# A two-layer hybrid encoder on one core: packed S5 preparation, layer 1's tables made beside other products, more half products, another order of steps

## The chip, the cores and the metric

The kernel runs on one core of one Trainium2 chip. The metric is the device time of one execution in microseconds (us). TensorE (PE in the profile) does the matrix products, VectorE (DVE), ScalarE (ACT) and GpSimd (POOL) the element-wise work, SyncE (SP) issues most of the DMAs and ScalarE the others.

## The reference, cut to what matters

```python
D_MODEL = 1024; SEQ = 512; DEPTH = 2; D_FF = 4 * D_MODEL
...
    lam_bar = jnp.exp(lam * step)                       # S5: 2 directions x 16 groups x 64 states
    b_bar = ((lam_bar - 1.0) / lam)[..., None] * b_c    # complex, (..., 16)
    bu = jnp.einsum('zgph,blgh->zblgp', b_bar, u.astype(jnp.complex64))
...
    for l in range(DEPTH):
        mix = hybrid_mixer(x, ...)      # x @ w_in, then S5, GLA, windowed attention, then @ w_out
        x = layer_norm(DEEPNORM_ALPHA * x + mix, ln1_g[l], ln1_b[l])
        hid = jnp.square(jax.nn.relu(x @ w_ff1[l]))
        x = layer_norm(DEEPNORM_ALPHA * x + hid @ w_ff2[l], ln2_g[l], ln2_b[l])
    return x
```

All data are float32. The S5 part is a diagonal complex recurrence in both directions; the kernel computes it in blocks of 8 steps with tables of powers of `lam_bar`, which depend on the parameters alone.

## The kernel before, in words

**Products.** A float32 product is made as three products of a fast 32-bit format (`mm3`, L250 to L252): each operand is split into a high and a low half. For weights `wunit` (L242 to L246) loads one 128x1024 unit into a buffer `raw` on SP's queue, copies the high half with ACT (L219) into one of six places of `WA`, and subtracts for the low half on DVE or POOL (L246). PE's products wait for that subtraction.

**A layer.** x stands in `XR` (512 tokens x 1024), transposed and split in `XT` (shown as XTP, XTQ, XTR). The input projection goes in four groups: wg1 (S5's u, GLA's values), g0 = wg0 (GLA's q, k and gates), g2 and g3 (attention). Then come the three mixers, the product with w_out in two halves (`out_half0`, `out_half1`), LayerNorm (`layer_norm`), the feed-forward part and a second LayerNorm.

**S5.** `tb_params` makes the powers of `lam_bar` up to 8, the factor (lam_bar-1)/lam (`QRI`) and the table `PS2` for both layers on DVE, at the start of the kernel. `tables(l)` goes over four groups j: it loads B and C (`BC`) and a second table (`CBK`), makes B times the factor (`BB`, six DVE operations of 128x64, L572 to L577), multiplies both with the powers (L587 to L595, each 128x512; for layer 0 the second of the two sets on POOL for j = 0 to 2), transposes on PE (`wst`, L599), writes one table to `scr_out` in HBM (L603), forms the block table on PE (`lag`, L607 to L613) and, after the last j, writes it to `scr_lag` in 15 small DMAs (L619, L621). `turns(l)` fills the rotation table `ROT`. `s5_u`, `s5_states`, `s5_scan` and `s5_out` use the tables.

**Feed-forward.** Chunk c (0 to 3) has eight tiles of 128 hidden units (`ff1`), then the product with w_ff2 in two halves. A plain tile is 24 matmuls of 128x512. From tile `CFG["st"][l]` on (12 in layer 0, 4 in layer 1), two tiles are made as a pair in seven products of halves (`ff1_pair`, 84 matmuls of 128x256, shown as f1s): its two weight tiles are loaded straight into `MA` (L1054, L1055), sums of their halves are made on DVE (L228) and split like other weights (ACT L219, DVE L1073).

**Order.** Within an engine the order is fixed when the program is built, by a list scheduler that takes the steps of the strings in `CFG["seq"]` as priorities. Layer 1's tables and turns are issued behind tile 3 of layer 0's chunk 0, at lower priority than what stands behind:

```python
            if l == 0 and c == 0:
                with tc.issue_after(state[CFG["tf"]].ins):
                    run(tables(1))
                    turns(1)
```

They use parts of `MA` and `MB`. Each queue (SP's and ACT's) issues its DMAs in order, and an issue that waits holds up what stands behind it. In the rows, `sc`, `pT` and `so` are attention's scores, transposed probabilities and outputs; `sy`, `zT`, `glg`, `glv` are the end of S5; `go`, `goT` the end of GLA.

Of the kernel before, what the change touches and what calls it, by code (L numbers as in the profile page):

```python
# [63 lines left out]
def trunk(tc, I, out, dbg=None):  # L64
# [299 lines left out]
    def tb_params():  # L364
# [3 lines left out]
        ST = [vs[:, 512:640], vs[:, 1536:1664]]  # L368
        tmps, IT = vs[:, 672:1024], vs[:, 1984:2048].bitcast(I32)
# [55 lines left out]
        V.tensor_scalar(e1, e1, -2.0, 1.0, op0=MUL, op1=ADD)  # L425
        V.tensor_copy(RW[:, 0], e1)
# [15 lines left out]

        tb = [t.rearrange("p (g k) -> p g k", g=32) for t in ST]

        def powers(W, b):
            def at(k):
                return W[:, 0, :, b + k], W[:, 1, :, b + k]
            for k, i, j in ((2, 1, 1), (3, 2, 1), (4, 2, 2)):
                cmul(*at(k), at(i), at(j))
            a4r, a4i = bc(W[:, 0, :, b + 4], 2, 4), bc(W[:, 1, :, b + 4], 2, 4)  # L450
            lo, hi_ = slice(b + 1, b + 5), slice(b + 5, b + 9)
            V.tensor_tensor(tb[0], W[:, 0, :, lo], a4r, op=MUL)
            V.tensor_tensor(tb[1], W[:, 1, :, lo], a4i, op=MUL)
# [11 lines left out]
        nr, (rr, ri) = t32(), (QRI[:, 0], QRI[:, 1])  # L465
        V.tensor_scalar(nr, PW[:, 0, :, 1], -1.0, None, op0=ADD)
        ni = PW[:, 1, :, 1]
        V.tensor_tensor(u1, are, are, op=MUL)
        V.tensor_tensor(u2, aim, aim, op=MUL)
        V.tensor_tensor(u1, u1, u2, op=ADD)  # L470
        V.reciprocal(e4, u1)
        V.tensor_tensor(u1, nr, are, op=MUL)
        V.tensor_tensor(u2, ni, aim, op=MUL)
        V.tensor_tensor(rr, u1, u2, op=ADD)
        V.tensor_tensor(rr, rr, e4, op=MUL)
        V.tensor_tensor(u1, ni, are, op=MUL)
        V.tensor_tensor(u2, nr, aim, op=MUL)
        V.tensor_tensor(ri, u1, u2, op=SUB)
        V.tensor_tensor(ri, ri, e4, op=MUL)
# [9 lines left out]
        unit_(wc, ws)  # L489
# [11 lines left out]
    def turns(l):  # L501

        t = [MA[:, 1024 * i:1024 * i + 1024] for i in range(2)]
        V.tensor_copy(ROT[:, :, :, 0], RW[:, :, 16 * l:16 * l + 16])
        k = 1
        while k < 64:
            n = 32 * k
            t1, t2 = [x[:, 0:n].rearrange("p (r g k) -> p r g k", r=2, g=16) for x in t]
            x = ROT[:, :, :, 0:k]
            wr, wi = [bc(bc(ROT[:, r, :, k - 1], 1, 2), 3, k) for r in range(2)]  # L510
            V.tensor_tensor(t1, x, wr, op=MUL)
            V.tensor_tensor(t2, x, wi, op=MUL)
            V.tensor_tensor(ROT[:, 0, :, k:2 * k], t1[:, 0], t2[:, 1], op=SUB)
            V.tensor_tensor(ROT[:, 1, :, k:2 * k], t1[:, 1], t2[:, 0], op=ADD)
            k *= 2
            if k == 8:
                unit_(ROT[:, 0, :, 7], ROT[:, 1, :, 7])

    def tables(l):
        nb = 2 if l == 0 else 1  # L520
        vs = M.yc[:, 2048:4096] if l == 0 else None
        areas = [MA, M.lt, MB] if l == 0 else [MA[:, 0:3072], MA[:, 5120:6656], MA[:, 3072:5120]]
# [12 lines left out]
        if l == 0:  # L535
            CBKs = [reg(512) for _ in range(nb)]
            BCs = [TAB[:, 256 * i:256 * i + 256] for i in range(4)]
# [16 lines left out]
        BCs = [c.rearrange("p (w r g h) -> p w r g h", w=2, r=2, g=4) for c in BCs]
# [472 lines left out]
    def ff_act(ps, i):  # L1027
# [12 lines left out]
        if i in (3, 4, 5, 7):  # L1040
            state["ff%d" % i] = ins
# [315 lines left out]
```

## Time and profile before

| what | value |
|---|---|
| median of 3 runs | 1258.68 us (1257.42 to 1258.88) |
| the profiled execution's own time | 1256.86 us |
| its span, first to last instruction | 1255.0 us |
| PE busy | 1182.3 us, 94% of the span |
| DVE, ACT, POOL busy | 888.9, 558.8, 150.4 us |
| mean granted TensorE clock | 0.973 of full speed |
| layer 0: input projection and mixers | about 0 to 240 us |
| layer 0: w_out, LayerNorm, feed-forward, LayerNorm | about 240 to 671 us |
| layer 1: the same two parts | about 671 to 845, 845 to 1255 us |

The span is what the profile covers; 1.9 us lie outside it. An engine's busy time is time in which it ran an instruction; the rest of the span it waited. PE's 94% is a mean over stages: in the feed-forward parts PE runs without a gap but one, in the mixers it waits in many small places. The granted clock says at what share of its full speed of 2.4 GHz TensorE's array ran.

### The profile page before, as it was taken

Reading aid. Unit: us, or ns where it says so; the run is one execution under the profiler, and the core shown is the slowest. Engines: PE = TensorE matmul, PEld = TensorE weight load, DVE = VectorE, ACT = ScalarE, POOL = GpSimd, SP = SyncE. Lnnn points to the kernel's source line nnn. Section 1 sums busy time; section 2 is a strip of 40 time slices with the busy share of each in tenths; the row PEclk is TensorE's granted clock in tenths of the full one; section 3 lists DMA queues with packets and bytes.
Section 4 is the critical chain, followed back from the end, with each engine's and each line's share of the span. In section 5 each row is a group of like instructions: output and inputs, shape, how many; then the busy total and the mean of one; then the engine's idle time right before and its main releaser. Section 6 shows DMA issues by size and latency. Waiting matters only on the chain.

```text
span 1255.0 us, 18704 instructions
## 1 busy us (share of the span) xinstructions
PE 1182.3 (94%) x7400; PEld 985.4 (79%) x7400; DVE 888.9 (71%) x1663; ACT 558.8 (45%) x939; POOL 150.4 (12%) x103
## 2 busy tenths in 40 slices
PE   6796899999999899999999999799999999999997
PEld 5685675668888788989987876456798898998986
DVE  8988768658876774856755278784997485764957
ACT  4262267525522442734623554572465272461640
POOL 3523112212000000000122131120300000000000
PEclk9898998999999899999999999899999999999999
DMA  6340430212442441421422414202144142250331
GB/s 221 107 143 9 122 106 1 80 56 76 134 160 97 146 148 42 143 85 53 131 103 57 161 60 102 84 17 84 35 138 148 51 146 74 87 164 19 101 119 67
DMA packets 50615, 121.67 MB, mean 97 GB/s; under 512 B 13280, under 2 KB 20320, under 8 KB 50528
## 3 DMA queue, kind: packets, MB, share of 16 engines
q1 hardware_dynamic: 37680, 103.53, 25.1%
q10 hardware_dynamic: 12848, 16.95, 4.9%
q8 instruction: 58, 0.95, 0.3%
q14 instruction: 29, 0.24, 0.1%
HBM read 110.53 MB, written 8.88 MB: 95 GB/s over the span
## 4 chain that ended last, share of the span: by engine, by line
PE 75%; DVE 16%; DMA 3%; ACT 2%; issue 2%; SPq 1%; ACTq 0%; POOL 0%; DVEq 0%
PE o L250 12%; PE o L251 11%; PE o L252 11%; PE f1s L250 6%; PE f1s L251 6%; PE f1s L252 6%; PE so L981 2%; PE proj L250 2%; PE proj L251 2%; PE proj L252 2%; PE pT L975 1%; PE f1e L251 1%; PE f1e L252 1%; PE f1e L250 1%; PE f L250 1%
## 5 line engine op out<-in xcount | busy, mean ns | idle before, releaser
L219 ACT ACTIVATE WA<-raw 128x1024 fp32r<-128x1024 f32 (+2 forms) x129 | 132.4, 1029 | 138.6 <-DMA raw<-in_w_ff 43.2
L246 DVE TENSOR_TENSOR WA<-raw,WA 128x1024 fp32r<-128x1024 f32 (+1 forms) x102 | 121.9, 1195 | 86.3 <-ACT WA L219 83.8
L219 ACT ACTIVATE WA<-MA 128x1024 fp32r<-128x1024 f32 (+1 forms) x72 | 64.6, 914 | 138.5 <-PE o L252 104.0
L992 DVE SCALAR_TENSOR_TENSOR XR<-XR,o 128x512 f32<-128x512 f32 (+1 forms) x81 | 52.9, 677 | 98.1 <-PE o L252 97.7
L1073 DVE TENSOR_TENSOR WA<-MA,WA 128x1024 fp32r<-128x1024 f32 (+1 forms) x72 | 74.5, 1043 | 16.5 <-ACT WA L219 16.5
L246 POOL TENSOR_TENSOR WA<-raw,WA 128x1024 fp32r<-128x1024 f32 (+2 forms) x27 | 62.0, 2301 | 173.0 <-ACT WA L219 162.1
L252 PE MATMUL f1s<-xs,WA 128*128 128x256 f32 x288 | 81.1, 281 | 0.0
L250 PE MATMUL f1s<-xs,WA 128*128 128x256 f32 x288 | 81.0, 281 | 0.0
L251 PE MATMUL f1s<-xs,WA 128*128 128x256 f32 x288 | 81.0, 281 | 0.0
L228 DVE TENSOR_TENSOR MA<-MA,f1s 128x256 f32<-128x256 f32 x120 | 49.1, 417 | 29.5 <-PE f1s L252 21.4
L228 POOL TENSOR_TENSOR XR<-XR,lt 128x512 f32<-128x512 f32 (+1 forms) x13 | 18.3, 1407 | 400.0 <-ACT XR L216 400.0
L250 PE MATMUL o<-WA,yYa 128*128 128x512 f32 (+1 forms) x162 | 64.4, 397 | 1.4 <-DVE XR L992 1.4
L250 PE MATMUL o<-WA,yQ 128*128 128x512 f32 (+1 forms) x164 | 64.2, 391 | 0.1
L251 PE MATMUL o<-WA,yQ 128*128 128x512 f32 (+1 forms) x164 | 64.1, 391 | 0.0
L250 PE MATMUL o<-WA,yP 128*128 128x512 f32 x160 | 63.8, 399 | 0.3 <-DVE yP L988 0.3
L251 PE MATMUL o<-WA,yYb 128*128 128x512 f32 (+1 forms) x162 | 63.8, 394 | 0.0
L252 PE MATMUL o<-WA,yYb 128*128 128x512 f32 (+1 forms) x162 | 63.6, 394 | 0.0
L250 PE MATMUL o<-WA,yYb 128*128 128x512 f32 (+1 forms) x162 | 63.5, 392 | 0.0
L251 PE MATMUL o<-WA,yYa 128*128 128x512 f32 (+1 forms) x162 | 63.5, 392 | 0.0
L252 PE MATMUL o<-WA,yYa 128*128 128x512 f32 (+1 forms) x162 | 63.5, 392 | 0.0
L252 PE MATMUL o<-WA,yQ 128*128 128x512 f32 (+1 forms) x164 | 63.4, 390 | 0.0
L251 PE MATMUL o<-WA,yP 128*128 128x512 f32 x160 | 63.4, 396 | 0.0
(456 smaller groups left out, 3534.2 us busy)
## 6 DMA issues: line engine op xcount, KB each, us to landing
raw<-in_w_ff SPq DMA_DIRECT2D x80, 512.0 KB, 3.4
MA<-in_w_ff SPq DMA_DIRECT2D x48, 512.0 KB, 3.5
raw<-in_wg SPq DMA_DIRECT2D x23, 512.0 KB, 3.5
raw<-in_w_out SPq DMA_DIRECT2D x16, 512.0 KB, 3.4
scr_out<-MA SPq DMA_DIRECT2D x8, 512.0 KB, 3.5
yc<-scr_out ACTq DMA_DIRECT2D x8, 512.0 KB, 4.8
raw<-in_wg SPq DMA_DIRECT2D x8, 288.0 KB, 2.8
MA<-in_s5cb ACTq DMA_DIRECT2D x8, 256.0 KB, 3.3
```

The costliest lines, as they stand in the source:

```text
L219: S.activation(out=o_, in_=i_, func=AF.Copy)
L228: eng.tensor_tensor(o_, a, b, op=op)
L246: (eng or V).tensor_tensor(WA[:, i, 1, c], raw[:, c], WAf[:, i, 0, c], op=SUB)
L250: T.matmul(ps, a[1], b[0], start=first, stop=False)
L251: T.matmul(ps, a[0], b[1], start=False, stop=False)
L252: T.matmul(ps, a[0], b[0], start=False, stop=last)
L975: T.transpose(ps[:, b * 128:b * 128 + 128], P[:, h, b * 128:b * 128 + 128], ident)
L981: T.matmul(ps[64 * v:64 * v + 64, :], av[:, tt - 1 + b0 + b, 64 * v:64 * v + 64], M.pT[v][:, b].rearrange("p h q -> p (h q)"), start=(b == ...
L992: V.scalar_tensor_tensor(x, x, scale, ps, op0=MUL, op1=ADD)
L1073: V.tensor_tensor(WA[:, u, 1, c], src, WAf[:, u, 0, c], op=SUB)
```

## The change

Four parts. (1) `tb_params` computes real and imaginary parts, and several powers, in one operation: the powers take 12 DVE operations of 64 to 256 columns where there were 24 of 32 and 128, the factor 14 where there were 16, and one correction (`unit_`, six operations) is left out. B and C of a layer come in one DMA of 512 KB, and the product with the factor is made for all groups at once: four DVE operations (two of 512, two of 256 columns) for 24 of 64. (2) Layer 1's tables are made in three parts: j = 0, 1 beside the second product of chunk 0, j = 2, 3 and the DMAs to `scr_lag` beside that of chunk 1, the turns beside that of chunk 2; they work in `MA[:, 2048:6656]` and `ROT`, and their turns in `MB`. (3) In layer 0 the pairs begin with tile 8: tiles 8 to 11 become two pairs. (4) The steps' order: layer 0 has `out` behind `scan` and `g3`, and `w3`, `y` ahead of `s5o`; layer 1 has `sink` ahead of `states`, and `out`, `y` behind `s5o`.

```diff
-    "st": [12, 4],
+    "st": [8, 4],
-    "seq": ["u g0 st0 tb st1 gates turns g2 scores states sink out scan g3 keys late w0 s5o w3 y w1 w2", "tb g0 u gates st0 st1 scan scores states sink g2 out g3 y keys late s5o w0 w2 w1 w3"],
+    "seq": ["u g0 st0 tb st1 gates turns g2 scores states sink scan g3 out keys late w0 w3 y s5o w1 w2", "tb g0 u gates st0 st1 scan scores sink states g2 g3 keys late s5o out w0 y w2 w1 w3"],
+    "td": [2, 2, 0, 0],
+    "tn": [0, 0, 7, 0],
...
+        def cmul(dst, a, br_, bi_):
+            t1, t2 = [v.rearrange("p r (g k) -> p r g k", g=32)[:, :, :, 0:a.shape[-1]] for v in (v1, v2)]
+            V.tensor_tensor(t1, a, br_, op=MUL)
+            V.tensor_tensor(t2, a, bi_, op=MUL)
+            V.tensor_tensor(dst[:, 0], t1[:, 0], t2[:, 1], op=SUB)
+            V.tensor_tensor(dst[:, 1], t1[:, 1], t2[:, 0], op=ADD)
+        for k in (1, 2, 4):
+            cmul(PW[:, :, :, k + 1:2 * k + 1], PW[:, :, :, 1:k + 1],
+                 *[bc(PW[:, r, :, k:k + 1].to_broadcast([128, 32, k]), 1, 2) for r in range(2)])
...
-        unit_(wc, ws)
...
-        areas = [MA, M.lt, MB] if l == 0 else [MA[:, 0:3072], MA[:, 5120:6656], MA[:, 3072:5120]]
+        areas = [MA, M.lt, MB] if l == 0 else [MA[:, 2048:6656], ROT.rearrange("p r g k -> p (r g k)")]
...
+        nc.scalar.dma_start(BC, I["s5bc"][l].rearrange("p (w r g h) -> p w r g h", w=2, r=2, g=16))
+        t3 = [t.rearrange("p (r g h) -> p r g h", r=2, g=16) for t in TT]
+        for t, q in zip(t3, (rr, ri)):
+            V.tensor_tensor(t, BC[:, 0], bc(bc(q, 1, 2), 3, 16), op=MUL)
+        V.tensor_tensor(BC[:, 0, 0], t3[0][:, 0], t3[1][:, 1], op=SUB)
+        V.tensor_tensor(BC[:, 0, 1], t3[0][:, 1], t3[1][:, 0], op=ADD)
         for j in range(4):
             yield j
...
-            V.tensor_tensor(t3[0], br, qr, op=MUL)
...
-            V.tensor_tensor(BB[:, 1], t3[0], t3[1], op=ADD)
...
-            if l == 0 and c == 0:
-                with tc.issue_after(state[CFG["tf"]].ins):
-                    run(tables(1))
-                    turns(1)
+            if l == 0:
+                if c == 0:
+                    tb1, tn1 = tables(1), turns(1)
+                with tc.issue_after(state["ff%d" % (8 * c + 7)].ins):
+                    for g, n in ((tb1, CFG["td"][c] + (c == 0)), (tn1, CFG["tn"][c])):
+                        if n:
+                            run(g, n)
```

**SP's queue in layer 0's feed-forward part, before.** `raw<-in_w_ff` are weight units (the 16 of one row: chunk 0's), `MA<-in_w_ff` the loads of the pairs, L603 and L619, L621 the tables' writes.

```order
33 L242 DMA raw<-in_w_ff 128x1024 x16
34 L603 DMA scr_out_95<-MA 128x1024
...
38 L603 DMA scr_out_95<-MA 128x1024 x2
39 L1054 DMA MA<-in_w_ff 128x1024
40 L619 DMA scr_lag_97<-MA 16x16x16 x2
41 L621 DMA scr_lag_97<-MA 16x16x16
...
53 L621 DMA scr_lag_97<-MA 16x16x16
54 L1054 DMA MA<-in_w_ff 128x1024
55 L1055 DMA MA<-in_w_ff 128x1024 x2
```

The same place in the changed kernel (the pairs' loads are L1030 and L1031, the tables' writes L580, L596 and L598):

```order
34 L244 DMA raw<-in_w_ff 128x1024 x8
35 L1030 DMA MA<-in_w_ff 128x1024
36 L1031 DMA MA<-in_w_ff 128x1024
37 L244 DMA raw<-in_w_ff 128x1024 x8
38 L580 DMA scr_out_95<-MA 128x1024 x2
39 L1031 DMA MA<-in_w_ff 128x1024
...
47 L244 DMA raw<-in_w_ff 128x1024 x7
48 L580 DMA scr_out_95<-MA 128x1024 x2
49 L1030 DMA MA<-in_w_ff 128x1024 x2
50 L1031 DMA MA<-in_w_ff 128x1024
51 L596 DMA scr_lag_97<-ROT 16x16x16 x2
...
64 L598 DMA scr_lag_97<-ROT 16x16x16
65 L1031 DMA MA<-in_w_ff 128x1024
```

The first pair's two loads now stand ahead of chunk 0's second weights and of every write of the tables, and the 15 writes to `scr_lag` have moved behind three of the four loads of chunk 2's first two pairs.

**DVE at the start, before**, from the last small operations of `tb_params` (L486 to L488) to the end of the first group's tables; the row of L246 with 576 columns is the third split of wg0.

```order
132 L577 TENSOR_TENSOR MB<-yc 128x64
133 L485 SCALAR_TENSOR_TENSOR yc<-RW 128x32
134 L486 TENSOR_TENSOR yc<-RW 128x32
135 L588 TENSOR_TENSOR yc<-PSR,MB 128x512
136 L487 TENSOR_SCALAR RW<-yc 128x32
137 L488 COPY RW<-yc 128x32
138 L246 TENSOR_TENSOR WA<-raw,WA 128x576
139 L494 TENSOR_TENSOR UNT<-RW 128x32
```

The same place in the changed kernel (L546 to L548 are the product of B with the factor, L564 to L572 the tables, L248 the split):

```order
112 L473 COPY RW<-yc 128x32
113 L546 TENSOR_TENSOR yc<-TAB,PSR 128x512
114 L488 COPY ROT<-RW 128x32
115 L547 TENSOR_TENSOR TAB<-yc 128x256
116 L548 TENSOR_TENSOR TAB<-yc 128x256
117 L572 SCALAR_TENSOR_TENSOR MA<-lt 128x4x128
118 L564 TENSOR_TENSOR yc<-PSR,TAB 128x512
119 L565 TENSOR_TENSOR yc<-PSR,TAB 128x512
120 L248 TENSOR_TENSOR WA<-raw,WA 128x576
121 L566 TENSOR_TENSOR MA<-yc 128x512
```

There are fewer small operations ahead of the split, and ahead of it now stand the product for all groups, L572 and two operations of the first table.

**PE in layer 0's mixers, before**: `go` is GLA's end, `sc` and `pT` attention's scores and transposed probabilities, `sy` S5's output.

```order
542 L951 LDWEIGHTS CB
543 L951 MATMUL sc<-CB 128x128
544 L832 MATMUL sy<-hx,lt 64x128 x2
545 L834 MATMUL sy<-yc 64x128 x4
...
550 L832 MATMUL sy<-hx,lt 64x128 x2
551 L834 MATMUL sy<-yc 64x128 x4
552 L946 MATMUL sc<-WA 128x256
...
568 L975 MATMUL pT<-CS,MA 128x128 x4
```

The same place in the changed kernel:

```order
554 L928 LDWEIGHTS CB
555 L928 MATMUL sc<-CB 128x128
556 L811 MATMUL sy<-yc 64x128
557 L952 MATMUL pT<-CS,MA 128x128 x8
558 L923 MATMUL sc<-WA 128x256
...
565 L926 MATMUL sc<-CB 128x128
566 L809 MATMUL sy<-hx,lt 64x128 x2
567 L811 MATMUL sy<-yc 64x128 x4
```

Half of `sy`'s rows now stand behind the first transposed probabilities and between later scores, where before all of them stood in one block ahead of those scores.

## Rows read from the trace of the kernel before

**Rows 1.** The page: busy times of the engines, and the chain that ended last.

```profile
PE 1182.3 (94%) x7400; PEld 985.4 (79%) x7400; DVE 888.9 (71%) x1663; ACT 558.8 (45%) x939; POOL 150.4 (12%) x103
...
PE 75%; DVE 16%; DMA 3%; ACT 2%; issue 2%; SPq 1%; ACTq 0%; POOL 0%; DVEq 0%
```

**Rows 2.** Windows: length, busy PE, PEld, DVE, ACT, POOL; clock, DMA share, GB/s.

```profile
40.00:60.00 20.00, 12.68 (x82) 11.34 (x81) 19.83 (x42) 4.26 (x8) 13.17 (x10) 0.74 0.33 111
...
80.00:100.00 20.00, 17.56 (x159) 14.61 (x157) 13.58 (x26) 15.54 (x27) 6.53 (x4) 1.00 0.32 113
...
180.00:200.00 20.00, 14.75 (x128) 12.73 (x125) 18.40 (x63) 13.62 (x39) 3.73 (x4) 0.74 0.33 106
...
800.00:850.00 50.00, 43.09 (x213) 25.71 (x214) 38.56 (x98) 31.18 (x85) 12.47 (x10) 0.90 0.04 11
```

**Rows 3.** Timeline of SP's queue, layer 0's chunk 1: start, duration, issue.

```profile
409.71 0.81 SPq L619 DMA_DIRECT2D scr_lag<-MA  x2
...
417.88 0.38 SPq L1054 DMA_DIRECT2D MA<-in_w_ff  x1
418.30 1.23 SPq L1055 DMA_DIRECT2D MA<-in_w_ff  x2
```

**Rows 4.** Timeline of DVE behind those loads; idle time before and its releaser in brackets.

```profile
423.59 0.69 DVE L228 TENSOR_TENSOR s<-MA 128x512 f32<-128x512 f32 x1 [2.17 <-DMA MA<-in_w_ff]
424.20 1.22 DVE L1073 TENSOR_TENSOR WA<-MA,WA 128x1024 fp32r<-128x1024 f32 x1
```

**Rows 5.** Timeline of PE: two matmuls of a plain tile, then the first pair.

```profile
415.02 0.40 PE L250 MATMUL f<-XTQ,WA 128*128 128x512 f32 x1
...
416.41 0.39 PE L250 MATMUL f<-XTQ,WA 128*128 128x512 f32 x1
...
425.48 0.58 PE L250 MATMUL f1s<-XTQ,WA 128*128 128x256 f32 x1 [5.41 <-DVE WA L1073]
```

**Rows 6.** Windows of PE alone in the pairs: length, busy (count), clock, DMA share, GB/s.

```profile
425.48:430.00 4.52, 4.52 (x21) 0.50 0.18 55
425.48:447.95 22.47, 22.47 (x169) 0.89 0.48 171
493.82:531.02 37.20, 37.20 (x314) 1.00 0.45 145
```

**Rows 7.** Windows of DVE alone at the start and in layer 0's chunk 0.

```profile
28.18:37.10 8.92, 8.57 (x42) 1.00 0.40 114
37.10:46.31 9.21, 9.14 (x25) 0.92 0.05 14
324.00:394.00 70.00, 55.45 (x101) 1.00 0.40 137
```

**Rows 8.** Timeline of DVE at the start: two small operations, the third split.

```profile
38.17 0.20 DVE L476 TENSOR_TENSOR yc<-yc,PSR 128x32 f32<-128x32 f32 x1
...
42.76 1.43 DVE L486 TENSOR_TENSOR yc<-RW 128x32 f32<-128x32 f32 x1
...
46.31 0.75 DVE L246 TENSOR_TENSOR WA<-raw,WA 128x576 fp32r<-128x576 f32 x1
```

**Rows 9.** Timeline of POOL in the same stretch.

```profile
37.13 1.06 POOL L587 TENSOR_TENSOR lt<-PSR,TAB 128x512 f32<-128x512 f32 x1 [11.15 <-DVE PSR L463]
...
42.75 1.40 POOL L246 TENSOR_TENSOR WA<-raw,WA 128x576 fp32r<-128x576 f32 x1
```

**Rows 10.** Timeline of PE at the start: the two matmuls that waited longest.

```profile
47.11 0.61 PE L251 MATMUL proj<-WA,XTQ 128*128 128x288 f32 x1 [5.18 <-DVE WA L246]
55.23 0.47 PE L599 MATMUL wst<-CS,MA 128*128 128x128 f32 x1 [2.15 <-DVE MA L593]
```

**Rows 11.** Timeline of PE in the mixers: matmuls that waited, layer 0, then layer 1.

```profile
189.41 0.58 PE L946 MATMUL sc<-WA 128*128 128x256 f32 x1 [3.83 <-ACT MA L216]
...
224.70 0.41 PE L975 MATMUL pT<-CS,MA 128*128 128x128 f32 x2 [2.60 <-DVE yYa L749]
...
804.30 0.45 PE L853 MATMUL zT<-CS,yb 128*128 128x128 f32 x1 [3.04 <-DVE SM__80 L961]
```

More of the change, by code (lines that the diff above doesn't have):

```diff
@@ L463, in tb_params @@
         V.tensor_copy(PS2[64:128, 1], PW[64:128, :, :, 8:0:-1])
[L465 to L470, printed above, removed]
-        V.reciprocal(e4, u1)
[L472 to L479, printed above, removed]
+        w1 = [v[:, :, 0:32] for v in (v1, v2)]
+        NR = tmps[:, nt[0] * 32:nt[0] * 32 + 64].rearrange("p (r g) -> p r g", r=2)
+        V.tensor_scalar(NR[:, 0], PW[:, 0, :, 1], -1.0, None, op0=ADD)
+        V.tensor_copy(NR[:, 1], PW[:, 1, :, 1])
+        ab = PRM[:, 0:64].rearrange("p (r g) -> p r g", r=2)
+        V.tensor_tensor(w1[0], ab, ab, op=MUL)
+        V.tensor_tensor(u1, w1[0][:, 0], w1[0][:, 1], op=ADD)
+        V.reciprocal(e4, u1)
+        V.tensor_tensor(NR, NR, bc(e4, 1, 2), op=MUL)
+        V.tensor_tensor(w1[0], NR, bc(are, 1, 2), op=MUL)
+        V.tensor_tensor(w1[1], NR, bc(aim, 1, 2), op=MUL)
+        V.tensor_tensor(QRI[:, 0], w1[0][:, 0], w1[1][:, 1], op=ADD)
+        V.tensor_tensor(QRI[:, 1], w1[0][:, 1], w1[1][:, 0], op=SUB)
         for k in range(3):
@@ L501, in turns @@
     def turns(l):
-        t = [MA[:, 1024 * i:1024 * i + 1024] for i in range(2)]
+        t = [MB[:, 512 * i:512 * i + 512] if l else MA[:, 1024 * i:1024 * i + 1024] for i in range(2)]
         V.tensor_copy(ROT[:, :, :, 0], RW[:, :, 16 * l:16 * l + 16])
@@ L506, in turns @@
         while k < 64:
[L507 to L514, printed above, removed]
+            yield k
+            for gs in [slice(0, 16)] if k < 32 or l == 0 else [slice(0, 8), slice(8, 16)]:
+                g = gs.stop - gs.start
+                t1, t2 = [x[:, 0:2 * g * k].rearrange("p (r g k) -> p r g k", r=2, g=g) for x in t]
+                x = ROT[:, :, gs, 0:k]
+                wr, wi = [bc(bc(ROT[:, r, gs, k - 1], 1, 2), 3, k) for r in range(2)]
+                V.tensor_tensor(t1, x, wr, op=MUL)
+                V.tensor_tensor(t2, x, wi, op=MUL)
+                V.tensor_tensor(ROT[:, 0, gs, k:2 * k], t1[:, 0], t2[:, 1], op=SUB)
+                V.tensor_tensor(ROT[:, 1, gs, k:2 * k], t1[:, 1], t2[:, 0], op=ADD)
             k *= 2
@@ L536, in tables @@
             CBKs = [reg(512) for _ in range(nb)]
-            BCs = [TAB[:, 256 * i:256 * i + 256] for i in range(4)]
+            BC = TAB
             TG = reg(1024).rearrange("p (r x) -> p r x", r=2)
@@ L541, in tables @@
             LL = reg(512)
-        BBs = [reg(128).rearrange("p (r g h) -> p r g h", r=2, g=4) for _ in range(nb)]
         if l == 0:
@@ L1214, in trunk @@
                  "g0": lambda: run(proj(I["wg0"][l], 288, evac_g0, "g1")), "gates": lambda: gla_gates(l),
[L1215 removed]
+                 "scan": lambda: s5_scan(l), "turns": lambda: l or run(turns(0)), "scores": lambda: gla_scores(l), "states": lambda: gla_states(l),
                  "sink": sink, "g2": lambda: run(proj(I["wg2"][l], 512, evac_g2, "g2")), "out": lambda: gla_out(l),
@@ L1310, in prepare @@
     bcx = np.stack([b, cc], 2)
-    r["s5bc"] = bcx.transpose(0, 4, 1, 2, 3, 5, 6).reshape(DEPTH, 4, 128, 256)
+    r["s5bc"] = bcx.reshape(DEPTH, 128, 1024)
     cp = cc.transpose(0, 3, 1, 4, 2, 5)
```

59 lines of the change are left out of this document (11 added, 48 removed).

## Prediction

> **What bounds the kernel now.** I read the page first. PE is busy for 94% of the span and holds 75% of the chain that ended last, DVE 16% [rows 1]. So time can be won in two ways only: fewer PE microseconds, or fewer of the 1255.0 - 1182.3 = 72.7 us in which PE waits. Next come the windows, which tell where it waits [rows 2]. Read PE's busy time against the length of each: 40 to 60 us has 7.3 us idle at a granted clock of 0.74, 180 to 200 has 5.25 at 0.74, 800 to 850 has 6.9 at 0.90. Then I read what each wait ended with: at the start DVE's work [rows 10], in the mixers ACT, DVE and a softmax that is late [rows 11], and in the feed-forward part one wait of 5.41 us, the longest of the kernel [rows 5]. The change touches all these places. A measurement of this kernel can tell some 0.2%, 2.5 us, from no change.
>
> **The feed-forward part of layer 0, the wait.** The chain is read backwards. The first pair's matmuls wait for DVE's split L1073; that follows the sums L228, which waited for a load into MA [rows 4]; the load was issued at 418.3, behind the writes to scr_lag that occupied SP's queue from 409.7 to 417.9 [rows 3]. So 8.2 us of small issues ahead of a 512 KB load make a wait of 5.41 us. After it PE is slow: 425.48 to 430 holds 21 matmuls at a granted clock of 0.50, that is 1.2 GHz, and the first 169 take 22.47 us, where 314 of the same kind take 37.20 later, 0.1185 each [rows 6]. 169 x 0.1185 = 20.0, so the slow clock costs 2.4. The wait is worth 5.4 + 2.4 = 7.8 us. In the new order the first pair's loads stand ahead of all the tables' writes, and the next chunk's small writes stand behind three of four loads. I take the whole 7.8. Late next could be the second load of chunk 2's second pair, still behind the 15 writes; it has a pair of PE's time (84 x 0.1185 = 10.0 us) and more as cover against the 8.2 us. If that load were late, the wait comes back: the bounds are 0 and 7.8.
>
> **Two pairs more.** Plain matmuls follow each other by (416.41 - 415.02) / 6 = 0.232 us [rows 5]; two plain tiles are 48 x 0.232 = 11.12, a pair 9.95. Two pairs save 2 x 1.17 = 2.3 us. The halves' sums and adds are DVE work, some 13 operations more for a pair than for two plain tiles, with a fifth of DVE's time free in this part (55.45 busy of 70) [rows 7].
>
> **Tables spread over the chunks.** The number of table operations falls, and they lie beside products on which PE has work of its own, so I cost them at nothing. The cover is PE's own stream: in chunk 0 of before they ran on DVE beside it. If it is gone, PE stands at a transpose or a block-table product that waits for DVE; one such wait is about two 512-column operations, 1.4 us at 0.69 [rows 4], and there are four groups: 0 to 5.6. I take 0. The sum of this part is -7.8 - 2.3 = -10.1, bounds -10.1 and +3.3.
>
> **The start.** PE waits 5.18 us for the third wg0 split, which DVE begins at 46.31, and 2.15 for the first table [rows 8, 10]. Ahead of the split DVE had 42 operations in 8.92 us and then 25 in 9.21 [rows 7], though a small one alone takes 0.20 [rows 8]: from 37.13 on POOL works on two-input operations [rows 9], and small DVE operations there take up to 1.43, as long as POOL's 1.40 beside it [rows 8, 9]. They hold each other up. The change takes out 14 operations ahead of that (24 to 12, 16 to 14): at most 14 x 0.20 = 2.8, and the rest are wider; I take 2.4, so DVE stands at 34.7 where it stood at 37.1. But the queue up to the split has changed too: 20 small operations (starts about 0.13 apart, 2.6 us) and eight wide ones (five of 512 columns at 0.69, two of 256 at about 0.4, the second split at 0.75: 5.0), 7.6 in all. That gives 42.3 with POOL silent. POOL's first five operations add 5 to 6 us as they did before, and the second group's first two may come before the split too, 2.1: 47.3 to 50.4, for 46.3. Of the 1 to 4 us lost, the wait of 2.15 at the first table takes back a part, since that table's last operation stands only four behind the split. I take +1.5, with +3.5 and, with POOL silent, -4 as bounds. From 60 to 80 us PE has no wait to give back, and from 80 to 100 DVE is idle for 6.4 of 20 us [rows 2]: a gain of DVE there ends in waiting for PE. That is why 40 fewer DVE operations bring me nothing here.
>
> **Other order of the mixers.** In layer 0 the first scores' softmax is moved ahead of GLA's end, so that half of sy's matmuls and the transposes fill the place in which PE waited 3.83 for ACT, and goT's wait of 2.60 moves behind other products [rows 11]. Bound: both gone, 6.4; none, or another wait in place, 0. I take half, -3. In layer 1 goT comes later, and zT and glg lie between other scores; the waits there sum to 6.9 in 50 us [rows 2], the largest 3.04 ahead of zT [rows 11]. Bounds +1 and -5; I take -3.
>
> **The sum**: -10.1 + 1.5 - 3 - 3 = -14.6 against the profiled execution's 1256.86 (span 1255.0 and 1.9 outside it): 1242.3. The median of the three runs lies 1.8 above that execution; half of that added gives 1243.
>
> **A rule that bears on it.** The row says: after the wait of 5.41 the granted clock was 0.50, and in the mixers, with waits spread about, it was 0.74 [rows 2, 6]. The Trainium skill, "TensorE: Matmul & The Clock Gate", Part 1, says that the throttled clock is the default and that activity releases it. My sum gives clock back only in the feed-forward part; by the rule, filled waits in the mixers would give clock back there too, and that is the third rival.
>
> **Rivals.**
>
> *Start late, mixers unchanged.* The waits in the mixers are of dependences (scores, exp, transpose, output), so a new order moves them and may not shorten them; DVE at 18.40 of 20 in 180 to 200 speaks for this [rows 2]. The start costs its full 3.5. Time: 1256.9 - 10.1 + 3.5 = 1250.3.
>
> *Slower than before: pairs and tables share MA.* Layer 1's tables now stand in MA[2048:6656], where pairs have loads, sums and partial results. Tables are made between chunks of pairs, so the loads of chunks 1 and 2 wait until the tables' writes to scr_out are done, and the next tables until the pairs are. It decides if the writes end less than a load and its split (418.3 to 425.5, 7.2 us) before PE needs the pair. Then the wait of 7.8 comes in both chunks where there was one: 1256.9 + 7.8 - 2.3 + 1.5 = 1263.9, with no gain in the mixers. Against it: a product of 192 matmuls (192 x 0.232 = 44.5 us) lies between two chunks' tiles, and only two of the four groups fall into each.
>
> *Waits and clock both come back.* In 180 to 200 PE's 14.75 busy at 0.74 would be 10.9 at full clock, 3.8 less, beside 5.25 idle; in 800 to 850 half of the idle 6.9 is 3.4, and half of 43.1 x 0.10 is 2.1. That makes 14.5 in place of my 6. Against it: chains of small operations, not PE, fill these windows. Time: 1242.3 - 8.5 = 1233.8.
>
> *The wait stays.* The feed-forward queue gets another blocked issue, once: 1242.3 + 7.8 = 1250.1.
>
> **How the numbers follow.** The forecast (1238 to 1247) 0.47; start late and mixers unchanged 0.22; waits and clock back 0.15; the wait stays 0.08; slower 0.08. The range takes in 1233.8 and the two cases at 1250, with the bounds of the start and tables above them: 1233 to 1254. All but the last case are faster by over 2.5 us, but a mixture of bounds (+3.3 or a start at +3.5 and mixers at +1) can eat a gain: faster 0.86, same 0.06, slower 0.08.
>
> **What would show it.** Right: no PE wait above 2 us before the first pair and a clock of 1.00 behind it; 84 f1s matmuls for tiles 8 and 9 in about 10 us; the third split of wg0 ending between 48 and 50, with PE's wait there longer than 5.18; the wait of 3.83 ahead of sc and that of 3.04 ahead of zT gone or halved. Wrong: a wait for a load into MA in chunk 1 or 2; a transpose wst that waits for DVE among products; new waits of like size in the mixers; or a start that ends earlier than before.

## The result and the profile after

The changed kernel takes 1243.97 us (median of 4 runs, 1239.0 to 1244.44) where the kernel before took 1258.2 beside it; the ratio (of the means) is 0.9878, 95% interval 0.9852 to 0.9904. By the medians that is 14.2 us, and the forecast was 1243. The profiled execution took 1244.44 us at a span of 1242.3.

To see where it went, both traces are cut at five matmuls that stand in both kernels: the first `gsc` (GLA's scores), which waits 4.10 us for ACT behind the gates; the first `f1e` (the first four tiles of a feed-forward part) in layer 0 that waits for DVE; the last transposes `xt` ahead of layer 1 that wait for DVE; the first `f1e` that waits in layer 1; and the end of the span.

| stage | before, us | after, us | difference | forecast |
|---|---|---|---|---|
| start, to the first `gsc` | 110.25 | 110.81 | +0.56 | +1.5 |
| layer 0's mixers, w_out, LayerNorm | 181.87 | 179.58 | -2.29 | -3 |
| layer 0's feed-forward part | 379.34 | 371.30 | -8.04 | -10.1 |
| layer 1's projections and mixers | 231.62 | 228.13 | -3.49 | -3 |
| layer 1's feed-forward part | 351.92 | 352.48 | +0.56 | 0 |
| sum (the spans) | 1255.0 | 1242.3 | -12.70 | -14.6 |

How much of such a difference one execution can show is seen in the kernels of the experiments. Five kernels with before's start and order of steps (before, e1, e5, e9, e12) have a start of 110.23 to 112.95, mean 111.2; five with the change's (after, e6, e7, e10, e11) have 110.75 to 111.84, mean 111.2: the start is worth nothing that these traces show. Layer 0's mixers are 181.26 to 182.26, mean 181.7, against 178.29 to 179.98, mean 179.2, and layer 1's 230.45 to 232.50, mean 231.4, against 226.87 to 228.37, mean 227.7: -2.6 and -3.8, with no overlap. Layer 1's feed-forward part has means of 352.6 and 352.4. With these means the sum is 0 - 2.6 - 8.0 - 3.8 - 0.2 = -14.6.

PE's windows of layer 0's two middle stages (length, busy and count, clock, DMA share, GB/s), the kernel before, then the changed one:

```profile
110.25:292.12 181.87, 164.89 (x922) 0.92 0.23 65
292.12:671.46 379.34, 371.61 (x2216) 0.99 0.34 111
...
110.81:290.39 179.58, 163.73 (x922) 0.94 0.26 70
290.39:661.69 371.30, 368.27 (x2288) 1.00 0.34 111
```

In the mixers PE's busy time fell by 1.2 us and its idle time by 1.1 (by the means of the ten traces 1.3 and 1.2), in the feed-forward part by 3.3 and 4.7. In layer 1's mixers the same view has 15.1 us of idle time before and 11.0 after, and a busy time of 216.5 and 217.1.

The page of the changed kernel, for [rows 1]:

```profile
PE 1177.4 (95%) x7472; PEld 982.2 (79%) x7472; DVE 895.2 (72%) x1626; ACT 564.2 (45%) x949; POOL 155.7 (13%) x103
...
PE 74%; DVE 17%; DMA 3%; ACT 3%; issue 2%; SPq 1%; DVEq 0%; ACTq 0%; POOL 0%
```

PE's idle time fell from 72.7 to 1242.3 - 1177.4 = 64.9 us and its busy time by 4.9. The windows of the changed kernel, with the columns of [rows 2]:

```profile
40.00:60.00 20.00, 12.33 (x88) 11.12 (x88) 19.73 (x31) 4.79 (x9) 13.35 (x9) 0.83 0.26 86
...
180.00:200.00 20.00, 16.83 (x182) 13.25 (x180) 19.59 (x69) 13.93 (x45) 4.30 (x5) 1.00 0.40 134
```

In 40 to 60 us PE waits about as long as before (7.7 for 7.3) and DVE is as full. In 180 to 200 us PE ran 182 matmuls where there were 128, at a clock of 1.00 where it was 0.74.

SP's queue in layer 0's feed-forward part of the changed kernel (start, duration, issue), for [rows 3]:

```profile
307.59 0.33 SPq L1030 DMA_DIRECT2D MA<-in_w_ff  x1
309.92 0.33 SPq L1031 DMA_DIRECT2D MA<-in_w_ff  x1
...
355.94 15.12 SPq L580 DMA_DIRECT2D scr_out<-MA  x2
...
471.68 1.09 SPq L1030 DMA_DIRECT2D MA<-in_w_ff  x2
472.88 0.36 SPq L1031 DMA_DIRECT2D MA<-in_w_ff  x1
477.64 0.82 SPq L596 DMA_DIRECT2D scr_lag<-ROT  x2
...
484.39 0.45 SPq L598 DMA_DIRECT2D scr_lag<-ROT  x1
484.93 0.39 SPq L1031 DMA_DIRECT2D MA<-in_w_ff  x1
```

and PE's window over chunk 1's pairs there (as [rows 6]):

```profile
390.80:428.24 37.44, 37.44 (x314) 1.00 0.37 122
```

The first pair's loads are issued at 308 to 310 us, 54 us before PE's first f1s at 363.7 (twelve of them stand among chunk 0's products), and the block of 312 matmuls in chunk 1 runs without a wait at full clock. The 15 small writes now end at 484.8, and the one load behind them did not come late. The waits of the changed kernel that answer to [rows 10] and [rows 11], PE's timeline:

```profile
49.09 0.61 PE L253 MATMUL proj<-WA,XTQ 128*128 128x288 f32 x1 [6.20 <-DVE WA L248]
...
50.90 0.47 PE L576 MATMUL wst<-CS,MA 128*128 128x128 f32 x1 [0.73 <-DVE MA L566]
...
156.47 2.07 PE L653 MATMUL gsc<-MA 128*128 128x512 f32 x2 [5.28 <-DVE MA L654]
...
189.06 0.30 PE L952 MATMUL pT<-CS,MA 128*128 128x128 f32 x1 [1.83 <-ACT MA L218]
...
545.66 0.50 PE L252 MATMUL o<-WA,yYa 128*128 128x512 f32 x1 [0.72 <-DVE XR L969]
...
787.91 0.30 PE L830 MATMUL zT<-CS,yb 128*128 128x128 f32 x1 [2.18 <-DVE GLS L296]
```

The third split costs a longer wait (6.20 for 5.18), the first table a shorter one (0.73 for 2.15). In the mixers 3.83 became 1.83, 3.04 became 2.18, and goT's wait of 2.60 in layer 0 is gone. Others are new or longer: 0.72 in chunk 2, where the turns now stand; 1.81 ahead of `qT` at 178.5, in all six kernels with the new order and the new preparation; and 5.28 ahead of a `gsc` that waited 3.39 before. The last one is 3.4 to 5.3 in the traces with the old order and 4.0 to 6.4 in those with the new, so its growth can't be put down to the order.

### The profile page after: what moved, and what is told of

Its sections match the earlier page's. It is cut to its first block, busy times and chain, and to the rows that moved or that the text cites. A ratio compares the mean times of both kernels' runs of the same rounds, so it can differ in the third digit from the quotient of the medians.

```text
span 1242.3 us, 18806 instructions
## 1 busy us (share of the span) xinstructions
PE 1177.4 (95%) x7472; PEld 982.2 (79%) x7472; DVE 895.2 (72%) x1626; ACT 564.2 (45%) x949; POOL 155.7 (13%) x103
## 4 chain that ended last, share of the span: by engine, by line
PE 74%; DVE 17%; DMA 3%; ACT 3%; issue 2%; SPq 1%; DVEq 0%; ACTq 0%; POOL 0%
PE o L252 11%; PE o L254 11%; PE o L253 11%; PE f1s L252 7%; PE f1s L254 7%; PE f1s L253 7%; PE proj L252 2%; PE so L958 2%; PE proj L253 2%; PE proj L254 2%; DVE WA L248 1%; PE pT L952 1%; PE f1e L253 1%; PE f1e L254 1%; PE f1e L252 1%
## 5 line engine op out<-in xcount | busy, mean ns | idle before, releaser
L221 ACT ACTIVATE WA<-raw 128x1024 fp32r<-128x1024 f32 (+2 forms) x125 | 128.3, 1028 | 143.3 <-PE o L254 48.0
L248 DVE TENSOR_TENSOR WA<-raw,WA 128x1024 fp32r<-128x1024 f32 (+1 forms) x98 | 118.7, 1211 | 76.3 <-ACT WA L221 76.1
L221 ACT ACTIVATE WA<-MA 128x1024 fp32r<-128x1024 f32 (+1 forms) x78 | 70.1, 914 | 131.0 <-PE o L254 94.1
L1049 DVE TENSOR_TENSOR WA<-MA,WA 128x1024 fp32r<-128x1024 f32 (+1 forms) x78 | 80.6, 1041 | 17.7 <-ACT WA L221 17.7
L254 PE MATMUL f1s<-xs,WA 128*128 128x256 f32 x312 | 87.9, 282 | 0.0
L253 PE MATMUL f1s<-xs,WA 128*128 128x256 f32 x312 | 87.8, 282 | 0.0
L252 PE MATMUL f1s<-xs,WA 128*128 128x256 f32 x312 | 87.8, 282 | 0.0
L248 POOL TENSOR_TENSOR WA<-raw,WA 128x1024 fp32r<-128x1024 f32 (+2 forms) x27 | 63.7, 2364 | 160.7 <-ACT WA L221 160.5
L230 DVE TENSOR_TENSOR MA<-MA,f1s 128x256 f32<-128x256 f32 x130 | 53.3, 416 | 30.0 <-PE f1s L254 20.8
```

The lines of the kernel that those rows point to most:

```text
L221: S.activation(out=o_, in_=i_, func=AF.Copy)
L230: eng.tensor_tensor(o_, a, b, op=op)
L248: (eng or V).tensor_tensor(WA[:, i, 1, c], raw[:, c], WAf[:, i, 0, c], op=SUB)
L252: T.matmul(ps, a[1], b[0], start=first, stop=False)
L253: T.matmul(ps, a[0], b[1], start=False, stop=False)
L254: T.matmul(ps, a[0], b[0], start=False, stop=last)
```

## The experiments

Times are medians; each ratio is to the kernel before, measured on the same chip, with its 95% interval. Differences to the changed kernel are between medians taken on different occasions; for e4, e6, e10 and e11 the intervals of the two ratios overlap, and the trace has to tell.

**e1, the writes on another queue** (the kernel before).

```diff
-            nc.sync.dma_start(dst[:, :, 14 - s], lg[rows, :, 0])
+            q_ = nc.scalar if l else nc.sync
+            q_.dma_start(dst[:, :, 14 - s], lg[rows, :, 0])
```

> The kernel before with one edit: layer 1's 15 small writes to scr_lag go out on ScalarE's queue instead of SP's; nothing else. Theory (the wait of 5.41 us ahead of layer 0's first pair is the order of SP's queue: loads blocked behind the writes): the pair's loads are issued before 410 us instead of at 418, no PE wait above 1 us ahead of f1s, granted clock 1.00 behind it, and the kernel is 7.8 us faster, about 1250.5. Rival 1 (the loads wait for the piece of MA that the last group's table holds): the wait stays within 1 us of 5.4 and the time at 1258. Rival 2 (only the queue changes: ScalarE's sequencer issues for 8 us and the split of the first pair's weights, which ScalarE begins, comes late instead): PE waits 2 to 5 us, the time is 1252 to 1256.

1258.78 us, ratio 1.0009 (0.9999 to 1.0019): no gain. SP's queue, what it waited for (us in total, times, longest), DVE and PE of this kernel (the queue's rows have start, duration, issue):

```profile
399.75 16.16 SPq L1055 DMA_DIRECT2D MA<-in_w_ff  x2
...
416.01 0.37 SPq L1056 DMA_DIRECT2D MA<-in_w_ff  x1
```

```profile
SPq L1055 <- DVE ROT L514: 15.4, 1, 15.4
```

```profile
414.83 0.69 DVE L514 TENSOR_TENSOR ROT<-MA 128x512 f32<-128x512 f32 x1
```

```profile
426.55 0.58 PE L250 MATMUL f1s<-XTQ,WA 128*128 128x256 f32 x1 [6.01 <-DVE WA L1074]
```

The two rows of L1055 span 16 us: with no small write ahead of them, the second still could not go before 416. The first of them belongs to the second pair, the second to the first pair. The latter waited 15.4 us for L514, the last operation of the turns, which reads its temporaries in MA[0:2048], the place of the first pair's weights. So the queue was not the cause by itself. The numbers are rival 1's, and its kind of cause too, though another user of MA than the one it named. That ScalarE's own issues (410.19 to 418.9) added to it was not separated.

**e2, the old order** (the changed kernel; `seq` as in the kernel before).

> The changed kernel with the steps' order of before (the strings of seq alone put back). Theory (the new order filled waits of PE in the mixers): the waits of 3.8, 2.6 and 3.0 us come back, the stretch from the first gsc to layer 1's first transposes grows by 2.9 us in layer 0 and by 3.5 to 5 in layer 1, the kernel is 6 us slower than the changed one, about 1250. Rival (the mixers' gain came from the packed preparation, or from where the clock gate fell): within 2 us of 1244.

1252.14 us, 0.9954 (0.9938 to 0.9970): 8 us slower than the changed kernel by the medians, somewhat more than expected. Layer 0's mixers take 183.44 us, layer 1's stage 231.97, and PE waits as before:

```profile
191.30 0.58 PE L923 MATMUL sc<-WA 128*128 128x256 f32 x1 [3.86 <-ACT MA L218]
```

So the gain of both mixers is the order's: 183.44 - 179.58 = 3.9 and 231.97 - 228.13 = 3.8. In layer 0 that is more than the whole stage gained, since e2's stage is 1.7 us longer than before's mean: something else in the change costs time there. Which part is open: e3, with the packed powers alone, has 183.22 too, but e8, the changed kernel without them, is longer than the changed one.

**e3, the packed powers alone** (the kernel before; `tb_params` of the change).

> The kernel before with the changed preparation alone (powers, factor, no correction; B and C are still loaded and multiplied by groups). Theory (DVE's gain at the start is eaten by the order on DVE and by POOL beside it, and DVE does not bind from 60 to 100 us): DVE's copies of the powers end 2 to 3 us earlier than at 37.1, the third split of wg0 ends between 46 and 50, the first gsc behind the gates starts within 1.5 us of 110.25, and the time is within 2 us of before's 1258. Rival (fewer operations shorten the start): the split ends before 45, the first gsc starts 3 us earlier, the time is 1254 or less.

1260.86 us, 1.0020 (1.0006 to 1.0035): a little slower. The third split ends at 46.4, and the first `gsc` starts at 111.64, inside the scatter of before's start. Waits went, others came: PE's timeline of e3

```profile
46.44 0.61 PE L251 MATMUL proj<-WA,XTQ 128*128 128x288 f32 x1 [3.81 <-DVE WA L246]
...
64.74 0.33 PE L595 MATMUL lag<-CS,MB 128*128 128x128 f32 x1 [2.10 <-DVE MB L594]
```

The rival (4 us faster) is out: fewer DVE operations at the start do not by themselves bring time.

**e4, the third split on POOL** (the changed kernel).

```diff
-    "g1": "VVVG",
+    "g1": "VVGG",
```

> The changed kernel with the third split of wg0 on POOL instead of DVE (one letter of g1). POOL's order then has it behind the first group's five operations, DVE's tables follow each other. Theory (the split's place in DVE's queue, behind seven wide operations that POOL holds up, makes the longest wait of the start, 6.2 us): the split ends at 43 to 45 instead of 49.0, PE's wait there falls to 1 to 3 us, the first table's transposes come no later than 50.9, and the kernel is 0 to 3 us faster than the changed one, 1241 to 1244; no more, because 60 to 100 us is bound by PE's own work and the chain through the gates. Rival (DVE and POOL hold each other up for the sum of their work, so that only the place of the wait moves): PE waits 4 to 6 us at the first table instead, the time is 1244 to 1246.

1246.22 us, 0.9908 (0.9887 to 0.9929): by the medians 2 us slower than the changed one, in no case faster. The split is done at 40.79 to 42.2, seven microseconds earlier, and PE stands at the tables instead:

```profile
40.79 1.43 POOL L248 TENSOR_TENSOR WA<-raw,WA 128x576 fp32r<-128x576 f32 x1
```

```profile
49.85 0.47 PE L576 MATMUL wst<-CS,MA 128*128 128x128 f32 x1 [7.18 <-DVE MA L566]
...
56.09 0.47 PE L576 MATMUL wst<-CS,MA 128*128 128x128 f32 x1 [2.73 <-DVE MA L570]
```

7.18 + 2.73 = 9.9 us for 6.20 + 0.73 + 0.74 = 7.7 (the second transposes wait 0.74 in the changed kernel). The rival holds, with a longer wait at the first table than its 4 to 6: here the place of the split in a queue only chose which matmul waits. The first `gsc` comes at 114.73, 3.9 us later, and layer 0's mixers give back 2.1 of that.

**e5, the turns' temporaries elsewhere** (the kernel before).

```diff
-        t = [MA[:, 1024 * i:1024 * i + 1024] for i in range(2)]
+        t = [MA[:, 4096 + 512 * i:4608 + 512 * i] if l else MA[:, 1024 * i:1024 * i + 1024] for i in range(2)]
...
+            for gs in [slice(0, 16)] if k < 32 or l == 0 else [slice(0, 8), slice(8, 16)]:
```

> The kernel before with one edit: layer 1's turns keep their temporaries in MA[4096:5120], in halves of 512, where no pair loads its weights; the queues are as before. Theory (what e1 left standing: the first pair's loads wait for the turns' last read of MA[0:2048], which ends at 415.0 us in the kernel before, and the queue's order only stacks on that): the two loads stand ahead of the 15 writes in SP's queue and are issued before 408 us, no PE wait above 1 us ahead of f1s, granted clock 1.00 behind it, the kernel is 6 to 8 us faster than before, 1250 to 1252. Rival (the queue alone): the time is the same as before's, 1258, or within 2 us.

1257.87 us, 0.9995 (0.9979 to 1.0011): no difference, by the time the rival's result. The trace tells more. The first pair's wait is gone, and the second pair has one. SP's queue and PE:

```profile
405.85 0.33 SPq L1055 DMA_DIRECT2D MA<-in_w_ff  x1
407.06 0.33 SPq L1056 DMA_DIRECT2D MA<-in_w_ff  x1
...
417.48 0.82 SPq L620 DMA_DIRECT2D scr_lag<-MA  x2
...
424.78 4.17 SPq L1056 DMA_DIRECT2D MA<-in_w_ff  x2
```

```profile
437.39 0.58 PE L250 MATMUL f1s<-xs,WA 128*128 128x256 f32 x1 [4.52 <-DVE WA L1074]
```

The next load to be late is the second pair's second one, behind the 15 writes.

**e6, pairs from tile 12** (the changed kernel; `"st": [12, 4]`).

> The changed kernel with the pairs of layer 0 beginning at tile 12 again; the tables stay spread over the chunks. Theory (two pairs save 2 x 1.17 us and nothing waits for them): layer 0's feed-forward part is 2.3 us longer, no wait ahead of f1s, the kernel is 2 to 3 us slower than the changed one, 1246 to 1247. Rival (the two pairs of chunk 1 cost waits of their own): the same time or faster, 1244 or less.

1246.22 us, 0.9897 (0.9881 to 0.9913): by the medians 2.3 us slower than the changed one. Layer 0's feed-forward part takes 374.01 us for 371.30 (370.5 to 372.1 in the five traces with pairs from tile 8 and spread tables). Two pairs are worth 2.7, forecast 2.3.

**e7, all tables in chunk 0** (the changed kernel; `"td": [4, 0, 0, 0]`, `"tn": [7, 0, 0, 0]`).

> The changed kernel with all of layer 1's tables and its turns put beside the second product of chunk 0 again; pairs from tile 8, areas as in the change. Theory (spreading is what makes room: four groups of tables and pairs share MA[2048:6656], and the 15 writes stand ahead of the second pair's loads): PE waits at the head of chunk 1, at wst or lag for DVE and at f1s for a load, 8 us or more in all with the slow clock behind it, the kernel is 8 to 15 us slower than the changed one, 1252 to 1259. Rival (the earlier order of the queue and the turns in MB are enough): within 3 us of 1244.

1269.12 us, 1.0079 (1.0063 to 1.0095): 25 us slower than the changed kernel, and slower than the one before. PE's waits in chunk 1, and SP's and DVE's rows ahead of them:

```profile
422.89 0.58 PE L252 MATMUL f1s<-xs,WA 128*128 128x256 f32 x1 [10.23 <-DVE WA L1049]
...
440.63 0.58 PE L252 MATMUL f1s<-XTQ,WA 128*128 128x256 f32 x1 [10.59 <-DVE MB L230]
```

```profile
413.06 0.45 SPq L1031 DMA_DIRECT2D MA<-in_w_ff  x1
```

```profile
439.50 0.42 DVE L500 TENSOR_TENSOR ROT<-MB 128x256 f32<-128x256 f32 x1
439.83 0.75 DVE L230 TENSOR_TENSOR MB<-MA,f1s 128x256 f32<-128x256 f32 x2
```

The first wait is the mechanism of the prediction's rival on the slow side: a pair's second load goes out at 413.06, behind the last table's write to `scr_out` (402.22), whose source lies at its destination, and behind the 15 small writes. The second wait is another: DVE makes the pairs' sum in `MB` only when the turns' last operation (L500) is done, and the turns have their temporaries in `MB`. Whether that place or the mere length of DVE's work holds it up, this run does not separate. So pairs from tile 8 go together with the tables and turns only because those are spread.

**e8, the old preparation** (the changed kernel; powers, factor and correction of before).

> The changed kernel with the powers, the factor and the correction of before, B and C still packed. Theory (from e3: packed powers alone made the stretch to the first gsc 1.4 us longer and the kernel 3 us slower, as the split of wg0 falls behind wide operations): the third split of wg0 ends before 47 us, the first gsc starts at 109.5 to 111, and the kernel is within 2 us of the changed one or faster, 1241 to 1245. Rival (fewer operations do help once B and C are packed): 2 to 4 us slower, 1246 to 1248.

1254.15 us, 0.9965 (0.9954 to 0.9977): 10 us slower than the changed kernel, against both theory and rival. The first `gsc` starts at 114.15, 3.3 us later, layer 0's mixers take 181.12, 1.5 more, and layer 1's feed-forward part 357.3, 4.9 more, though the edit is 800 us ahead of it. (The cut there falls earlier in e8's order of work; both stages of layer 1 together are 3.4 us longer than the means above.)

```profile
924.60 0.36 PE L252 MATMUL f1s<-XTR,WA 128*128 128x256 f32 x1 [2.68 <-ACT MA L221]
```

In that far stage ACT's, DVE's and PE's work stands in another order than in the changed kernel, though the edit is to the start alone. So a part's worth is not the difference that its removal makes, and e3 and e8 can't be added.

**e9, turns elsewhere and the writes on GpSimd's queue** (the kernel before; e5's edit, and e1's with `nc.gpsimd`).

> The kernel before with both edits: the turns' temporaries out of the pairs' loads (as e5), and the 15 writes to scr_lag on GpSimd's queue, which is idle there (e1 had them on ScalarE's). Theory (the wait has two causes that stack, the area that the turns read until 415 us and the queue behind the writes until 418; each alone only moves it): no PE wait above 1 us ahead of any f1s of chunk 1, granted clock 1.00 through chunk 1, layer 0's feed-forward part 6 to 8 us shorter than before's 379.3 us, the time 1250 to 1252. Rival (a third cause, for instance DVE's load with the tables and turns in chunk 1): a wait of 3 us or more stays, the time is 1255 or more.

1261.68 us, 1.0033 (1.0021 to 1.0044): slower. The writes end on POOL's queue at 429.4, and the second pair still waits (SP's queue, and what this issue waited for):

```profile
431.16 0.33 SPq L1057 DMA_DIRECT2D MA<-in_w_ff  x1
```

```profile
SPq L1057 <- DMA scr_lag<-MA: 6.4, 1, 6.4
```

```profile
443.08 0.58 PE L250 MATMUL f1s<-xs,WA 128*128 128x256 f32 x1 [7.56 <-DVE WA L1075]
```

The last load of that pair is held 6.4 us, with no write ahead of it in its queue, until the writes have read: their source, `LL`, lies in MA[3072:3584], inside that pair's second weights, MA[3072:4096]. The theory of two causes was incomplete: each pair has an area of its own that it waits for.

**e10, pairs from tile 4** (the changed kernel; `"st": [4, 4]`).

> The changed kernel with the pairs of layer 0 beginning at tile 4, as in layer 1. Theory (from e6: a pair is worth 1.1 to 1.4 us where nothing waits for it; the tables begin only after chunk 0's tiles): 2 to 3 us faster than the changed kernel, 1241 to 1242. Rival (in chunk 0 the loads of two pairs come beside the first weights, and the last sums of LayerNorm's transposes must be ready earlier): PE waits 2 us or more ahead of the first f1s, 1244 or slower.

1247.55 us, 0.9915 (0.9900 to 0.9929): by the medians 3.6 slower than the changed one. The rival holds: the first pair waits in chunk 0.

```profile
323.87 0.55 PE L252 MATMUL f1s<-XTQ,WA 128*128 128x256 f32 x1 [3.66 <-DVE WA L1049]
```

**e11, the turns divided** (the changed kernel; `"tn": [0, 0, 4, 3]`).

> The changed kernel with layer 1's turns divided between chunk 2 (four steps) and chunk 3 (three). Theory (the turns' DVE work makes PE wait 0.7 us for the sum XR at the second product of chunk 2, where there was no wait before): that wait goes, chunk 3 hides the rest, 0.5 to 1 us faster than the changed kernel, 1243 to 1244. Rival (chunk 3 has LayerNorm's work on DVE behind it): the last transposes ahead of layer 1 come later, 1244 to 1246.

1242.04 us, 0.9876 (0.9860 to 0.9893). The wait of 0.72 is gone and layer 0's feed-forward part takes 370.49 for 371.30. By the time it can't be told from the changed kernel.

**e12, areas apart** (the kernel before; queues and order strings untouched; the turns' last step goes in two halves, as in e5).

```diff
-        t = [MA[:, 1024 * i:1024 * i + 1024] for i in range(2)]
+        t = [MA[:, 5504 + 512 * i:6016 + 512 * i] if l else MA[:, 1024 * i:1024 * i + 1024] for i in range(2)]
...
-        areas = [MA, M.lt, MB] if l == 0 else [MA[:, 0:3072], MA[:, 5120:6656], MA[:, 3072:5120]]
+        areas = [MA, M.lt, MB] if l == 0 else [MA[:, 0:3072], MA[:, 5120:6656], MA[:, 4096:5120]]
```

> The kernel before with areas alone changed: layer 1's block table and the source of the 15 writes lie in MA[4096:5120], the turns' temporaries in MA[5504:6528], so that nothing of the tables lies where the first two pairs load their weights longer than the last group's own tables. Queues, pairs, tables' place and order strings are as before. Theory (after e1, e5 and e9: each of two areas held one pair's loads, MA[0:2048] by the turns and MA[3072:3584] by the writes, and SP's order followed from that): all four loads of the two pairs stand ahead of the 15 writes and are issued by 408 us, no PE wait above 1.5 us ahead of any f1s of chunk 1, layer 0's feed-forward part is 371.5 to 374 us for before's 379.3, and the kernel is 5 to 8 us faster than before. Rival (there is a further cause, DVE's load of tables, turns and sums in one place): a wait of 3 us or more stays and the time is within 3 us of before's.

1251.5 us, 0.9942 (0.9925 to 0.9958): 7.0 us faster than before, by memory places (the halves alone gained nothing in e5). SP's queue, and PE's windows around the former wait and over the whole feed-forward part:

```profile
311.08 0.33 SPq L1056 DMA_DIRECT2D MA<-in_w_ff  x1
...
398.30 0.33 SPq L1056 DMA_DIRECT2D MA<-in_w_ff  x1
400.61 3.91 SPq L1055 DMA_DIRECT2D MA<-in_w_ff  x2
413.17 0.82 SPq L620 DMA_DIRECT2D scr_lag<-MA  x2
```

```profile
395.00:440.00 45.00, 45.00 (x291) 1.00 0.52 161
293.25:664.73 371.48, 369.17 (x2215) 1.00 0.35 113
```

All four loads of the first two pairs go ahead of the writes, the second pair's second one, whose place nobody else uses now, already at 311. PE has no wait, the clock stays at full, and the feed-forward part takes 371.48 us: 7.86 less than before's 379.34. PE's idle time there falls from 7.7 to 2.3 us and its busy time from 371.6 to 369.2, the 5.4 and the 2.4 of which the prediction made its 7.8. The writes stand on the same queue as before; free of a place to wait for, the scheduler put the loads ahead of them.

## Why the prediction was right, and where it was not

**The feed-forward wait, 7.8 us: the size was right, the cause was named too narrowly.** The step that failed is "the load was issued at 418.3, behind the writes to scr_lag that occupied SP's queue". The rows showed an order in a queue and nothing of why it was so. Three things were in the way: the queue's order, the turns' temporaries and the writes' source. e1 took away the first, e5 the second, e9 both, and none gained time; e12 took away the second and third, left the queue alone and gained all of it. The pairs' weights could not be loaded while the turns' temporaries and the writes' source lay in their places; the queue's order followed from that. The change clears both places (turns in `MB` and two chunks later, the writes' source in `ROT`, no table in MA[0:2048]), as well as moving the writes. So it was in part luck that the whole 7.8 came: the new order of the queue, which the prediction counted on, brought nothing alone (e1). The prediction looked at `MA` only for the changed kernel, as a rival, and not for the kernel before.

**Two pairs, 2.3:** e6 shows 2.7.

**Tables at nothing: the mis-sized term.** 7.86 + 2.3 is 10.2, and the part gained 8.0. Of the missing 2.2 us, 0.72 is PE's new wait for DVE beside the turns (gone in e11). Another 1.1 is the pairs' own pace: the blocks of 312 matmuls took 37.44, 37.3 and 37.4 us for 37.0 before (from the first row of a block to the next product), at a full granted clock. This is not the tables' doing: e1 and e9, kernels of before with the tables where they were, have 37.44 too, and e5 and e12 have 37.0. What makes them 1% slower is open, and the last 0.4 is not accounted for. So of this term only the 0.72 is shown; the prediction's bounds, 0 to 5.6, hold it.

**The start, +1.5:** +0.56 in one trace, none by the means. The forecast of the split (a start at 47.3 to 50.4, an end between 48 and 50) was just met, with 47.43 and 49.0, and so was the point that the wait at the first table gives it back (2.15 fell to 0.73). DVE's row for that split shows the mechanism that was counted on, an operation that took 0.75 us before and 1.60 here, beside POOL's L565 (1.50 us from 46.92) and L248 (1.92 from 48.38):

```profile
47.43 1.60 DVE L248 TENSOR_TENSOR WA<-raw,WA 128x576 fp32r<-128x576 f32 x1
```

**The mixers, -3 and -3:** -2.6 and -3.8 by the means, and e2 shows that they are the order's. The rival "waits and clock both come back" was half seen: in 180 to 200 us the clock came back to 1.00 from 0.74, but the stage gained 2.6 us, not the 9 that the rival counted there. The Trainium skill, "TensorE: Matmul & The Clock Gate", Part 1, has activity release the throttle; the trace agrees, with 182 matmuls there where 128 stood. But over the whole stage the clock rose only from 0.92 to 0.94, which goes with the 1.2 us of busy time that PE saved, and the idle time fell by no more than 1.1, since other waits grew. So about half of this term's gain was busy time, which the prediction's sum had left out in the mixers, and half shorter waits, from which it had expected all.

**Rivals.** "Start late, mixers unchanged" is out by both its halves. "Pairs and tables share MA" came as a wait of loads and not of PE. Chunk 2's first pair lies in MA[0:2048], where the tables do not work: PE's first products of that chunk, which need it, already stand at 455.13. The loads at 471.7 to 473.2, and the one at 484.9 behind the 15 writes, belong to the second and third pairs (the prediction and the section on the change count them to the first two). One of them had waited for the block table's product:

```profile
SPq L1030 <- PE lag L587: 4.2, 1, 4.2
```

PE stood at none of them. e7 shows this rival come true once, with 10.2 us of PE's time, where the prediction priced it at 7.8 in each of two chunks; e7's other wait, 10.6, is of the turns.

The sum was nearer than its terms, and that is luck: the feed-forward part was forecast 2.1 us too good and layer 0's mixers 0.4, the start 1.5 too bad, layer 1's mixers 0.8 and its feed-forward part 0.2 too modest.

## What to carry to other kernels

When a transfer starts late behind others in its queue, ask what it could not have started before: look up whose data lies at its destination, and when that was last read. Moving the queue's entries gave nothing here (e1, and e9 with the turns moved as well); moving two temporaries by some kilobytes gave 7 of the 14 us (e12). Where a scheduler sets the order, price a part by the wait that it takes away in the trace, not by one removal alone: the packed powers added to the kernel before made it 3 us slower (e3), and taken from the changed kernel made that 10 us slower (e8).

## What the runs showed that was not expected

The same wait can cost the clock or not. In every kernel PE waits 1.84 to 1.89 us for DVE ahead of the last transposes of layer 0, and the same twelve `proj` matmuls follow. Windows of PE over these twelve, first in the changed kernel, then in the kernel before (length, busy, clock, DMA share, GB/s):

```profile
662.16:666.53 4.37, 4.37 (x14) 0.62 0.38 108
```

```profile
671.87:674.73 2.86, 2.86 (x15) 1.00 0.59 165
```

By rows of the timeline the twelve took 4.3 to 4.6 us in six kernels (after, e1, e2, e7, e9, e11) and 3.0 in the other eight, with waits of the same length. So 1.5 us of a comparison of two single executions can be the clock alone. It is in the table above: layer 1's 228.13 of the changed kernel holds it, the 231.62 before does not. The Trainium skill's same page says (Part 1, "What's actually happening") that the point of the change varies, since the gate's watch does not begin with the kernel's work; the traces agree that it varies, here between a change of level and none; that this is the reason here, no run shows.
